# Both matrix products of each gated MLP by Strassen's seven half-size products, in a two-layer decoder step

## The chip, the cores and the metric

The kernel runs on one core of a Trainium2 chip. A core has five engines with a queue of instructions each: PE (matrix products, 128 by 128, results into PSUM), DVE (elementwise), ACT (elementwise with functions), POOL (elementwise, cannot read PSUM) and SP (issues DMA transfers). The metric is the device time of one execution in microseconds. Before the change it is 2903.1 us, the median of 3 runs (2901.17 to 2904.2).

## The reference

One inference step of two layers on 1024 prompt positions and 8 single-token samples, 1032 rows of 1024 features together, in float32. Layer 0 mixes positions with gated linear attention and sparse attention, layer 1 with an mLSTM. Behind each mixer stands the part that changes, a gated MLP with a causal convolution of width 3 on the gate:

```python
def _conv_ffn(xn, w_up, conv_w, conv_b, w_down, conv_state):
    t = xn.shape[1]
    gpre, up = jnp.split(xn @ w_up, 2, axis=-1)            # 1024 -> 2 x 2816
    full = jnp.concatenate([conv_state.astype(gpre.dtype), gpre], axis=1)
    acc = conv_b + full[:, 0:t] * conv_w[0]
    for j in range(1, CONV_W):
        acc = acc + full[:, j:j + t] * conv_w[j]
    h = jax.nn.gelu(acc) * up
    return h @ w_down, full[:, full.shape[1] - (CONV_W - 1):]  # 2816 -> 1024

xp = xp + d      # residual; at the end a final RMSNorm
```

## The kernel before, in words

The stream x is kept transposed: 8 tiles of 128 features by 1032 columns (1024 prompt positions and 8 samples), each as a pair `xh`, `xl` (a high part that PE takes as float32r, and the rest). A product of float32 numbers is made of three: high weight by high x, high by low, low by high. `product_steps` (L250) issues them for each 128-row block k of the input: 3 parts times 3 column groups of 344 (`GW`), so 9 matmuls per block.

`ffn` (L398) goes through the 22 inner feature tiles f. For each it makes the gate tile (72 matmuls of 344 columns), applies the convolution (L428 on ACT, L429 and L430 on DVE), the GELU (L432, L433 on ACT) and the factor `rstd` of the RMSNorm (L435 on POOL), then makes the up tile (72 matmuls) and multiplies it in (L440), and splits the result into `hh` and `hl` (L443, L444). Behind every 4 (or 3) inner tiles stands the down product of these: 8 output tiles, each added to `acc` (L458). In layer 1 the last 3 inner tiles are done by `finish` (L519), column group by column group, with the final norm and the output behind each.

A weight tile of 128 output columns is fetched on SP's queue (`load_w`, L223), multiplied by the norm's gain on POOL (L235, up weights only), and split into a high part on ACT (L236) and a low part on DVE (L237). `wraw` and `wspl` have two buffers each. PSUM holds two buffers of three banks for the products (`fpp`) and two banks for small things (`fpm`).

Each mixer ends in `out_project` (L358), whose output tile m is added to the stream (L392, L394) and split again by `split_x` (L343), which also squares it on ACT; `add_sq` (L166) sums the squares on POOL, and `make_rstd` (L189) makes `rstd` of the sum within the first gate tile's work.

The order on each queue is not that of the program text: a planner orders the traced instructions of each engine by their place in the text and by when it takes them to be ready. It places semaphore waits for every true dependence, for tile buffers too. Instructions of one engine then run in the planned order.

Of the kernel before, what the change touches and what calls it, by code (L numbers as in the profile page):

```python
# [14 lines left out]
PSUM = bass.MemoryType.PSUM  # L15

T = 1024
NS = 8
# [7 lines left out]
EPS = 1e-6  # L26

# [16 lines left out]
def grp(ap):  # L44
    return ap.rearrange("p (g t) -> p g t", g=NG)


class Trunk:
# [22 lines left out]
    def setup(self):  # L71
        nc, a = self.nc, self.a
        self.const = c = self.pool("const", 1)
        self.xp = self.pool("xp", 1)
# [10 lines left out]
        self.xh = [self.xp.tile([128, TT], F32R, name=f"xh{k}") for k in range(KD)]  # L85
        self.xl = [self.xp.tile([128, TT], F32R, name=f"xl{k}") for k in range(KD)]
        self.rstd = self.vec.tile([128, TT], F32, name="rstd")
        self.gains = c.tile([128, 56], F32, name="gains")

# [76 lines left out]
    def add_sq(self, sq, k):  # L166
        nc = self.nc
        if k == 0:
            self.sq = self.vec.tile([128, TT], F32, name="sq")
            nc.gpsimd.tensor_copy(self.sq, sq)  # L170
        else:
            (nc.vector if k == KD - 1 else nc.gpsimd).tensor_tensor(self.sq, self.sq, sq, op=OP.add)
# [67 lines left out]
    def project(self, pp, w, xh, xl, m=128):  # L240

        pt = pp.tile([128, NG, 512], F32, name="pp")
        self.products([pt[:m, g, :GW] for g in range(NG)], w, xh, xl)
        return pt

    def products(self, outs, w, xh, xl, ks=None):
        for _ in self.product_steps(outs, w, xh, xl, ks):
            pass

    def product_steps(self, outs, w, xh, xl, ks=None):  # L250
        nc = self.nc
        wh, wl = w
        kt = len(xh)
        for k in range(kt):
            kw = ks[k] if ks else k
            for i, (l, r) in enumerate(((wh, xh), (wh, xl), (wl, xh))):
                for g in range(NG):
                    nc.tensor.matmul(outs[g], l[:, kw, :], r[k][:, g * GW:(g + 1) * GW],  # L258
                                     start=(k == 0 and i == 0), stop=(k == kt - 1 and i == 2))
            if k < kt - 1:  # L260
                yield

    def stacked_steps(self, outs, w, xh, xl):

        nc = self.nc
        for k in range(KD):
            for m, x in ((128, xh), (64, xl)):
                for g in range(NG):
                    nc.tensor.matmul(outs[g][:m], w[:, k, :m], x[k][:, g * GW:(g + 1) * GW],  # L269
                                     start=(k == 0 and m == 128), stop=(k == KD - 1 and m == 64), skip_group_check=True)  # L270
            if k < KD - 1:
                yield
# [70 lines left out]
    def split_x(self, k, x):  # L343
# [5 lines left out]
        self.add_sq(x, k)  # L349
# [8 lines left out]
    def out_project(self, w, split, ks, ready, late, nat=None):  # L358
# [3 lines left out]
        with self.tp(name="opp", bufs=2, space=PSUM) as pp, \  # L362
# [15 lines left out]
            head = [begin(0)]  # L378
            self.take(head[0][1], ready)
            head.append(begin(1))  # L380
# [7 lines left out]
            for m in range(KD):  # L388
                pt, steps = head[m] if m < 2 else begin(m)
                self.take(steps, KD)  # L390
                x = self.rstd if m % 2 else self.vec.tile([128, TT], F32, name="sq_t")
                nc.vector.tensor_tensor(grp(x), pt[:, :, :GW], grp(self.xh[m].bitcast(F32)), op=OP.add)  # L392
                eng = nc.vector if m == KD - 1 else nc.gpsimd
                eng.tensor_tensor(x, x, self.xl[m].bitcast(F32), op=OP.add)  # L394
                self.split_x(m, x)


    def ffn(self, l, last):  # L398
        nc, a, tc = self.nc, self.a, self.tc
        parts = (4, 4, 4, 4, 3, 3)  # L400
        gain = self.gains[:, 16 + 8 * l:24 + 8 * l]
        w_up, w_dn = a["ffn_w_up"][l], a["ffn_w_down"][l]
        with self.tp(name="facc", bufs=1) as fa, self.tp(name="fh", bufs=5) as fh, \
                self.tp(name="ft", bufs=2) as ft, self.tp(name="f1", bufs=1) as f1:
            acc = [fa.tile([128, TT], F32, name=f"acc{m}") for m in range(KD)]
            with self.tp(name="fpp", bufs=2, space=PSUM) as pp, self.tp(name="fpm", bufs=2, space=PSUM) as self.ps:
                f0 = 0
                for pi, n in enumerate(parts):
                    hh, hl = [], []
                    final = last and pi == len(parts) - 1  # L410
                    if final:
                        spare = [(fh.tile([128, TT], F32R, name="hh"), fh.tile([128, TT], F32R, name="hl")) for _ in range(2)]
                    w = w_dn[f0 * 128:(f0 + n) * 128]
                    for f in range(f0, f0 + n):
                        pg = self.project(pp, self.split_w([(0, w_up[:, f * 128:(f + 1) * 128])], KD, gain), self.xh, self.xl)
                        if f == 0:
                            self.make_rstd(self.bank)
                            taps, st, cvp, cvs = self.conv_setup(l, f1)
                        g = ft.tile([128, 2 + T + 3 * NS], F32, name="g")
                        gs = g[:, 2 + T:].rearrange("p (b j) -> p b j", j=3)  # L420
                        nc.gpsimd.memset(g[:, 0:2], 0.0)
                        nc.gpsimd.tensor_copy(gs[:, :, 0:2], st[:, :, :, f])
                        self.scale_cols(g[:, 2:2 + T], gs[:, :, 2], pg)
                        nc.gpsimd.tensor_copy(cvp[:, :, f], g[:, T:T + 2])
                        nc.gpsimd.tensor_copy(cvs[:, :, :, f], gs[:, :, 1:3])
                        n3 = T + 3 * NS
                        h = ft.tile([128, n3], F32, name="cv")
                        nc.scalar.activation(h, g[:, 0:n3], AF.Identity, bias=taps[:, 66 + f:67 + f], scale=taps[:, f:f + 1])  # L428
                        nc.vector.scalar_tensor_tensor(h, g[:, 1:1 + n3], taps[:, 22 + f:23 + f], h, op0=OP.mult, op1=OP.add)  # L429
                        nc.vector.scalar_tensor_tensor(h, g[:, 2:2 + n3], taps[:, 44 + f:45 + f], h, op0=OP.mult, op1=OP.add)  # L430
                        u = ft.tile([128, TT], F32, name="u")
# [4 lines left out]
                        pu = self.project(pp, self.split_w([(0, w_up[:, DFF + f * 128:DFF + (f + 1) * 128])], KD, gain),  # L436
                                          self.xh, self.xl)
                        if final and f == f0 + n - 1:
                            wts = [self.last_weight(w, n, m, spare[m // 2]) for m in range(4)]
                        nc.vector.tensor_tensor(grp(u), pu[:, :, :GW], grp(u), op=OP.mult)  # L440
                        th = fh.tile([128, TT], F32R, name="hh")
                        tl = fh.tile([128, TT], F32R, name="hl")
                        nc.scalar.activation(th, u, AF.Copy)  # L443
                        nc.vector.tensor_tensor(tl, u, th, op=OP.subtract)  # L444
                        hh.append(th)
                        hl.append(tl)
                    if final:
                        break
                    for m in range(KD):
                        if (pi, m) == (len(parts) - 1, 5):  # L450
                            self.conv_store(l, cvp, cvs, ft)
                        pt = self.project(pp, self.split_w([(0, w[:, m * 128:(m + 1) * 128])], n), hh, hl)
                        ga = grp(acc[m])
                        if pi == 0:
                            nc.vector.tensor_tensor(ga, pt[:, :, :GW], grp(self.xh[m].bitcast(F32)), op=OP.add)
                            nc.gpsimd.tensor_tensor(acc[m], acc[m], self.xl[m].bitcast(F32), op=OP.add)
# [1494 lines left out]
```

## Time and profile before

| | before |
|---|---|
| median of 3 runs | 2903.1 us |
| profiled execution | 2923.18 us, span 2921.4 us |
| PE busy | 2843.8 us (97%), 17827 matmuls |
| DVE, ACT, POOL busy | 1394.3, 855.8, 788.7 us |
| mean granted clock of PE | 0.991 |
| layer 0's MLP | about 904 to 1674 us |
| layer 1's MLP with the final norm | about 2152 to 2921 us |

All times of the profile are of the one profiled execution, in microseconds from the span's start. Busy times of an engine are unions of its instructions; matmuls overlap each other in them, so the pace of a stream of matmuls is read from starts, not from durations.

### The profile page before, as it was taken

To read this page: it belongs to the slowest core of one execution; us is meant where nothing else is said; L and a number is where in the kernel's file an instruction comes from. 1 tells how busy PE (TensorE), PEld (TensorE's weight loads), DVE (VectorE), ACT (ScalarE), POOL (GpSimd) and SP (SyncE) were. 2 spreads that over 40 slices of the span, in tenths; PEclk is the share of its full clock that TensorE was granted. 3 is DMA by queue.
4 is the path that set the end of the run, shared out by engine and by line. 5 is a ranking of instruction groups with operands and counts; after the bars stand their busy time and mean duration, and the time that the engine had idled before them with its cause. 6 is when DMAs were issued, how large, how long until landed. Compare 5 with 4: busy or idle time off the path is not lost.

```text
span 2921.4 us, 41871 instructions
## 1 busy us (share of the span) xinstructions
PE 2843.8 (97%) x17827; PEld 2592.8 (89%) x17827; DVE 1394.3 (48%) x2111; ACT 855.8 (29%) x1353; POOL 788.7 (27%) x623
## 2 busy tenths in 40 slices
PE   7899999999999999999999999999999999999999
PEld 7677544687799999999999998889999999999998
DVE  6456775447555333433333764435553433333335
ACT  4333444333443221212122422323432212121224
POOL 3430223431134241313122411110343413131223
PEclk9999999999899999999999999999999999999999
DMA  6420010551111121111111212221111112111112
GB/s 184 146 80 23 1 58 1 175 179 37 38 45 47 33 62 37 55 40 49 54 31 55 56 44 60 60 66 48 44 50 37 55 37 58 44 48 48 36 55 80
DMA packets 252478, 171.92 MB, mean 59 GB/s; under 512 B 28878, under 2 KB 240949, under 8 KB 252229
## 3 DMA queue, kind: packets, MB, share of 16 engines
q1 hardware_dynamic: 237692, 128.36, 15.2%
q0 software_dynamic: 9728, 33.56, 3.4%
q10 hardware_dynamic: 4872, 7.33, 0.7%
q8 instruction: 140, 2.29, 0.3%
q14 instruction: 46, 0.37, 0.0%
HBM read 156.02 MB, written 17.38 MB: 59 GB/s over the span
## 4 chain that ended last, share of the span: by engine, by line
PE 91%; DVE 5%; ACT 1%; issue 1%; DMA 1%; POOL 0%; another core or an unknown queue 0%; SPq 0%; DVEq 0%; ACTq 0%; POOLq 0%
PE pp L258 56%; PE ps L258 14%; PE ps L1059 2%; PE pd L258 2%; PE ps L814 1%; PE pd L962 1%; PE ps L535 1%; PE ps L802 1%; PE pd L1028 1%; PE pd L1029 1%; DVE wl L237 1%; PE ps L1211 1%; PE ps L1813 1%; PE ps L1220 1%; PE ps L269 1%
## 5 line engine op out<-in xcount | busy, mean ns | idle before, releaser
L236 ACT ACTIVATE wh<-wr 128x1024 fp32r<-128x1024 f32 (+2 forms) x240 | 213.3, 889 | 1066.0 <-PE pp L258 880.5
L235 POOL TENSOR_TENSOR wr<-wr,gains 128x1024 f32<-128x1024 f32 x132 | 257.3, 1950 | 856.3 <-issue 250.1
L258 PE MATMUL pp<-xh,wh 128*128 128x344 f32 x2112 | 448.4, 321 | 0.0
L258 PE MATMUL pp<-xl,wh 128*128 128x344 f32 x2112 | 448.2, 320 | 0.0
L258 PE MATMUL pp<-xh,wl 128*128 128x344 f32 x2112 | 446.4, 319 | 0.0
L258 PEld LDWEIGHTS pp<-xl,wh 128*128 128x128 f32 x2112 | 357.4, 189 | 0.0
L258 PEld LDWEIGHTS pp<-xh,wh 128*128 128x128 f32 x2112 | 355.5, 188 | 0.4
L258 PEld LDWEIGHTS pp<-xh,wl 128*128 128x128 f32 x2112 | 351.9, 188 | 0.0
L237 DVE TENSOR_TENSOR wl<-wr,wh 128x1024 fp32r<-128x1024 f32 (+2 forms) x238 | 267.6, 1124 | 10.5 <-ACT wh L236 10.4
L258 PE MATMUL ps<-xh,wh 128*128 128x344 f32 x960 | 224.5, 339 | 3.2 <-ACT wh L236 1.9
L258 PE MATMUL ps<-xl,wh 128*128 128x344 f32 x960 | 215.0, 327 | 1.1 <-issue 0.6
L258 PE MATMUL ps<-xh,wl 128*128 128x344 f32 x960 | 212.1, 326 | 2.6 <-DVE wl L237 1.4
L258 PE MATMUL pp<-hh,wl 128*128 128x344 f32 x984 | 208.0, 319 | 0.7 <-DVE wl L237 0.7
L258 PE MATMUL pp<-hl,wh 128*128 128x344 f32 x984 | 208.5, 320 | 0.0
L258 PE MATMUL pp<-hh,wh 128*128 128x344 f32 x984 | 207.7, 320 | 0.0
L469 DVE TENSOR_TENSOR g<-pp,rstd 128x688 f32<-128x688 f32 x44 | 38.5, 875 | 311.1 <-PE pp L258 310.9
L458 DVE TENSOR_TENSOR acc<-pp,acc 128x1032 f32<-128x1032 f32 x72 | 88.7, 1232 | 196.8 <-PE pp L258 196.8
L440 DVE TENSOR_TENSOR u<-pp,u 128x1032 f32<-128x1032 f32 x44 | 54.2, 1232 | 257.0 <-PE pp L258 238.3
L258 PEld LDWEIGHTS ps<-xh,wh 128*128 128x128 f32 x960 | 163.5, 192 | 11.3 <-issue 6.0
L258 PEld LDWEIGHTS ps<-xl,wh 128*128 128x128 f32 x960 | 164.9, 192 | 6.6 <-issue 5.6
L258 PEld LDWEIGHTS ps<-xh,wl 128*128 128x128 f32 x960 | 163.5, 191 | 5.7 <-issue 3.6
L258 PEld LDWEIGHTS pp<-hh,wl 128*128 128x128 f32 x984 | 164.6, 188 | 1.2 <-DVE wl L237 1.2
(704 smaller groups left out, 4483.6 us busy)
## 6 DMA issues: line engine op xcount, KB each, us to landing
wr<-in_ffn_w_up_dram SPq DMA_DIRECT2D x88, 512.0 KB
wr<-in_ffn_w_down_dram SPq DMA_DIRECT2D x64, 256.0 KB
wr<-in_odd_w_in_dram SPq DMA_DIRECT2D x24, 512.0 KB
wr<-in_even_w_in_dram SPq DMA_DIRECT2D x18, 512.0 KB
wr<-in_ffn_w_down_dram SPq DMA_DIRECT2D x32, 192.0 KB
kv<-in_cache_win_kv_dram SPq DMA_DIRECT2D x8, 512.0 KB
cst<-in_state_mlstm_c_dram SPq DMA_DIRECT2D x16, 256.0 KB
out_dram<-cst SPq DMA_DIRECT2D x16, 256.0 KB
```

Of the source, the lines that this page charges most:

```text
L235: self.gain_eng.tensor_tensor(raw, raw, gain[:, :, None].to_broadcast([128, kt, m]), op=OP.mult)
L236: nc.scalar.activation(wh, raw, AF.Copy)
L237: nc.vector.tensor_tensor(wl, raw, wh, op=OP.subtract)
L258: nc.tensor.matmul(outs[g], l[:, kw, :], r[k][:, g * GW:(g + 1) * GW], start=(k == 0 and i == 0), stop=(k == kt - 1 and i == 2))
L269: nc.tensor.matmul(outs[g][:m], w[:, k, :m], x[k][:, g * GW:(g + 1) * GW], start=(k == 0 and m == 128), stop=(k == KD - 1 and m == 64), sk ...
L440: nc.vector.tensor_tensor(grp(u), pu[:, :, :GW], grp(u), op=OP.mult)
L458: nc.vector.tensor_tensor(ga, pt[:, :, :GW], ga, op=OP.add)
L469: nc.vector.tensor_tensor(dst[:, :2 * GW].rearrange("p (g t) -> p g t", g=2), pt[:, :2, :GW], self.rstd[:, :2 * GW].rearrange("p (g t) -> ...
L535: nc.tensor.matmul(pt, l[:, k, :], r[k][:, s], start=(k == 0 and i == 0), stop=(k == n - 1 and i == 2))
L802: nc.tensor.transpose(pt[:, j * 128:(j + 1) * 128], kv[:, half * 4 + j, sl * 256 + c * 128:sl * 256 + c * 128 + 128], self.ident)
L814: nc.tensor.matmul(hid[c][64 * h:64 * h + 64, :273], wt[:, c, q], xt[h][:, q, :273], start=(g == 0 and q == 0), stop=(g == 7 and q == 3))
L1059: nc.tensor.matmul(po[64 * g:64 * g + 64], v[:, kb, 64 * g:64 * g + 64], p[:, g * 512:(g + 1) * 512], start=first, stop=last)
```

## The change

Each MLP product is cut in two along inputs, outputs and columns, and done by Winograd's form of Strassen's algorithm: seven products of halves instead of eight. The columns are two halves of `HW` = 516, each two matmuls of `QW` = 258. One unit of weights makes one gate tile and its up tile (or the output tiles j and j+4): `factors` fetches both weight tiles, makes seven combined weights of half the rows and splits each in its high and low part, into a ring of five buffers. `combine` makes the seven combinations of x, once for each layer, into 28 slots that take the place of `xh`, `xl`. The seven products accumulate in three PSUM pairs of banks in the order a, b, a, b, c, b, c:

```diff
+    def combine(self, i, b, slot, pool):
+        b11, b12, b21, b22 = b
+        eng = nc.gpsimd if pool else nc.vector
+        if i == 1:
+            eng.tensor_tensor(b12, b22, b12, op=OP.subtract)
+            eng.tensor_tensor(b11, b11, b12, op=OP.add)
+        elif i == 4:
+            eng.tensor_tensor(b21, b21, b11, op=OP.subtract)
+            eng.tensor_tensor(b11, b22, b11, op=OP.subtract)
+        src = self.halves((b11, b11, b21, b12, b11, b21, b22)[i])
+        nc.scalar.activation(slot[:, 0, :, :QW], src, AF.Copy)
+        (nc.gpsimd if pool == 2 else nc.vector).tensor_tensor(slot[:, 1, :, :QW], src, slot[:, 0, :, :QW], op=OP.subtract)
+
+    def factors(self, srcs, kt, gain):
+        raws = [p.tile([128, KD, 128], F32, name=x)[:, :2 * kt] for p, x in ((self.wraw, "wr"), (ext, "wr2"))]
+        for raw, src in zip(raws, srcs):
+            nc.sync.dma_start(raw, src.rearrange("(k p) f -> p k f", p=128))
+        yield
+        if gain is not None:
+            for raw in raws:
+                nc.gpsimd.tensor_tensor(raw, raw, gain[:, :, None].to_broadcast([128, 2 * kt, 128]), op=OP.mult)
+        (a11, a12), (a21, a22) = ((r[:, :kt], r[:, kt:]) for r in raws)
+        ...
+        yield parts(a11)          # parts: high on ACT, low on DVE, kt x 128 columns each
+        nc.gpsimd.tensor_tensor(s1, a21, a22, op=OP.add)
+        nc.gpsimd.tensor_tensor(s2, s1, a11, op=OP.subtract)
+        yield parts(s2)
+        yield parts(a12)
+        nc.gpsimd.tensor_tensor(a11, a11, a21, op=OP.subtract)
+        yield parts(a11)
+        yield parts(s1)
+        yield parts(a22)
+        nc.gpsimd.tensor_tensor(a12, a12, s2, op=OP.subtract)
+        yield parts(a12)
+
+    def seven(self, pp, stream, rhs, after):
+        banks = {}
+        for i, x in enumerate("ababcbc"):
+            while len(self.ahead) < 4:
+                ...                                  # the next weights of the stream
+            hi, lo = self.ahead.popleft()
+            new = x not in banks
+            if new:
+                banks[x] = pp.tile([128, 2, 512], F32, name=f"pp{x}", bufs=1)
+            pt, right = banks[x][:, :, :QW], rhs(i)
+            for k, r in enumerate(right):
+                for n, (w, part) in enumerate(((hi, 0), (hi, 1), (lo, 0))):
+                    for q in range(2):
+                        nc.tensor.matmul(pt[:, q], w[:, k], r[:, part, q, :QW], start=(new and k == 0 and n == 0), ...)
+            after(i, pt)
```

All 22 inner tiles come first now. `t` and `u2` are the halves of one tile that is allocated once for the MLP. What follows the seven products of tile f:

```diff
+                def begin():
+                    ...
+                    nc.vector.tensor_tensor(self.halves(g[:, 2:2 + HW]), c11, self.halves(self.rstd[:, :HW]), op=OP.mult)
+                def after(i, pt):
+                    if i == 0:
+                        nc.scalar.copy(self.halves(t), pt)
+                        ...                          # f == 0: make_rstd
+                    elif i == 1:
+                        v.tensor_tensor(self.halves(u2), pt, self.halves(t), op=OP.add)
+                    elif i == 2:
+                        c11 = pt
+                    elif i == 3:
+                        u3 = self.vec.tile([128, TT], F32, name="sq")[:, :HW]
+                        v.tensor_tensor(self.halves(u3), pt, self.halves(t), op=OP.add)
+                    elif i == 4:
+                        v.tensor_tensor(self.halves(u3), pt, self.halves(u3), op=OP.add)
+                    elif i == 5:
+                        v.tensor_tensor(self.halves(t), pt, self.halves(t), op=OP.add)
+                    if i == (2 if f else 6):
+                        begin()
+                    if i == 6:
+                        v.tensor_tensor(self.halves(u2), pt, self.halves(u2), op=OP.add)
+                        nc.gpsimd.tensor_tensor(g[:, 2 + HW:2 + T], u2[:, :T - HW], self.rstd[:, HW:T], op=OP.mult)
+                        nc.gpsimd.tensor_tensor(gs[:, :, 2], u2[:, T - HW:], self.rstd[:, T:], op=OP.mult)
                         ...                          # convolution and GELU as before: ACT, DVE, DVE, ACT
                         nc.gpsimd.tensor_tensor(u, u, self.rstd, op=OP.mult)
+                        v.tensor_tensor(u[:, :HW], u[:, :HW], t, op=OP.mult)
+                        v.tensor_tensor(u[:, HW:], u[:, HW:], u3, op=OP.mult)
+                        nc.sync.dma_start(hid[f], u)
```

The inner tiles go to DRAM (`hid`) and come back as chunks of 6, 6, 6 and 4 tiles (layer 1: 6, 6, 6, and the last 4 in `finish`); the stream itself goes to DRAM (`res`) in `out_project` and comes back ahead of the down products. `turn` combines a chunk: for the first chunk within the last inner tile, for the others within the last output pair of the chunk before.

```diff
+            def first(i):                            # combinations of x, within f == 0
+                for j in range(4):
+                    self.combine(i, xs[j], right[4 * i + j], j < 3)
+                return right[4 * i:4 * i + 4]
+            def turn(i, n):
+                comb[i] = [self.slot(6 + 3 * i + p) for p in range(n // 2)]
+                for p in range(n // 2):
+                    self.combine(i, quads(raw[p], raw[p + n // 2]), comb[i][p], 1 + p // 2)
...
+            for c, (f0, n) in enumerate(chunks):
+                ...
+                for j in range(4):
+                    ...
+                    def after(i, pt):
+                        if i == 0:
+                            nc.scalar.copy(self.halves(t), pt)
+                        elif i == 1:
+                            v.tensor_tensor(self.halves(u2), pt, self.halves(t), op=OP.add)
+                            p.tensor_tensor(u2, u2, a12, op=OP.add)
+                        elif i == 3:
+                            v.tensor_tensor(self.halves(u3), pt, self.halves(t), op=OP.add)
+                            p.tensor_tensor(u3, u3, a22, op=OP.add)
+                            p.tensor_tensor(t, t, a21, op=OP.add)
+                        else:
+                            to, x = {2: (a11, a11), 4: (a22, u3), 5: (a21, t), 6: (a12, u2)}[i]
+                            v.tensor_tensor(self.halves(to), pt, self.halves(x), op=OP.add)
+                        if j == 3 and nxt and not (last and c == len(chunks) - 1):
+                            turn(i, nxt[1])
+                    self.seven(pp, stream, lambda i: used[i], after)
...
+            self.open_x()                            # layer 0: xh, xl are made again behind the MLP
+            for m in PAIRS:
+                self.split_x(m, big[:, m])
```

One tile `big` of 8 by 1032 columns holds the stream, the MLP's work areas, and the buffers that the mixers had in tiles of their own (`oN`, `oT`, `kv`, `nat`, `p` and others). The order of the stream's tiles in `out_project` and behind layer 0's MLP is `PAIRS` = 0, 4, 1, 5, 2, 6, 3, 7.

## Rows read from the trace of the kernel before

**Rows 1.** The page: busy times; the chain of work that ended last, by engine.
```profile
PE 2843.8 (97%) x17827; PEld 2592.8 (89%) x17827; DVE 1394.3 (48%) x2111; ACT 855.8 (29%) x1353; POOL 788.7 (27%) x623
PE 91%; DVE 5%; ACT 1%; issue 1%; DMA 1%; POOL 0%; another core or an unknown queue 0%; SPq 0%; DVEq 0%; ACTq 0%; POOLq 0%
```
**Rows 2.** Windows of both MLPs: length, busy per engine (instructions), clock, DMA share, GB/s.
```profile
903.80:1674.00 770.20, 766.14 (x4831) 763.50 (x4830) 327.82 (x328) 175.55 (x203) 213.01 (x175) 1.00 0.17 48
2152.00:2921.00 769.00, 762.64 (x4842) 759.03 (x4841) 319.62 (x375) 180.52 (x233) 209.71 (x173) 1.00 0.17 50
```
**Rows 3.** Timeline of PE, matmuls of 344 columns, 39 from first to last row.
```profile
1395.42 0.63 PE L258 MATMUL pp<-xl,wh 128*128 128x344 f32 x3
...
1401.58 0.64 PE L258 MATMUL pp<-xh,wl 128*128 128x344 f32 x3
```
**Rows 4.** Timeline of PE, matmuls of 264 columns, 7 from first to last row.
```profile
2904.87 0.28 PE L535 MATMUL ps<-hl,xh 128*128 128x264 f32 x1
...
2905.72 0.29 PE L535 MATMUL ps<-hh,xl 128*128 128x264 f32 x1
```
**Rows 5.** Timeline of one gate tile: next product's first matmul, then what follows.
```profile
963.21 0.64 PE L258 MATMUL pp<-xh,wh 128*128 128x344 f32 x3
...
963.41 0.88 DVE L469 TENSOR_TENSOR g<-pp,rstd 128x688 f32<-128x688 f32 x1 [7.69 <-PE pp L258]
...
964.81 1.27 ACT L428 ACTIVATE cv<-g,taps 128x1048 f32<-128x1048 f32 x1 [0.81 <-DVE g L472]
...
966.11 1.31 DVE L429 SCALAR_TENSOR_TENSOR cv<-g,taps,cv 128x1048 f32<-128x1048 f32 x1 [0.21 <-ACT cv L428]
...
970.04 2.41 POOL L435 TENSOR_TENSOR u<-u,rstd 128x1032 f32<-128x1032 f32 x1 [0.88 <-ACT u L433]
```
**Rows 6.** Lines by form: elementwise instructions, busy and mean ns.
```profile
L440 DVE TENSOR_TENSOR u<-pp,u 128x1032 f32<-128x1032 f32 x44 | 54.2, 1232 | 257.0 <-PE pp L258 238.3 <-POOL u L435 18.6
L471 DVE TENSOR_TENSOR g<-pp,rstd 128x336 f32<-128x336 f32 x44 | 21.9, 497 | 0.0
L1085 POOL TENSOR_TENSOR co<-co,cf 128x512 f32<-128x512 f32 x8 | 10.2, 1277 | 61.0 <-DVE cf L1083 61.0
L235 POOL TENSOR_TENSOR wr<-wr,gains 128x1024 f32<-128x1024 f32 x14 | 26.7, 1904 | 36.9 <-DMA wr<-in_ffn_w_up_dram 32.0 <-issue 3.5 <-DVE u L440 1.4
```
**Rows 7.** Source L237 and L236, 1000 to 1040 us: ns min/median/max.
```profile
L237 DVE TENSOR_TENSOR wl<-wr,wh x7: 679/682/2736, 1004.3 to 1038.5; 128x512 fp32r<-128x512 f32 x6, 128x1024 fp32r<-128x1024 f32 x1
L236 ACT ACTIVATE wh<-wr x7: 632/632/1060, 1002.7 to 1036.9; 128x512 fp32r<-128x512 f32 x6, 128x1024 fp32r<-128x1024 f32 x1
```
**Rows 8.** Timeline of DVE and POOL; source L444, L440: ns min/median/max.
```profile
937.56 1.90 POOL L235 TENSOR_TENSOR wr<-wr,gains 128x1024 f32<-128x1024 f32 x1 [1.36 <-DVE u L440]
938.60 1.95 DVE L444 TENSOR_TENSOR hl<-u,hh 128x1032 fp32r<-128x1032 f32 x1 [1.13 <-ACT hh L443]
L444 DVE TENSOR_TENSOR hl<-u,hh x44: 1232/1234/2010, 938.6 to 2870.4; 128x1032 fp32r<-128x1032 f32 x44
L440 DVE TENSOR_TENSOR u<-pp,u x44: 1232/1232/1233, 936.2 to 2868.1; 128x1032 f32<-128x1032 f32 x44
```
**Rows 9.** Timeline of PE where the first MLP's `rstd` is made.
```profile
915.33 1.32 PE L196 MATMUL ps<-sq,ones 128*128 128x344 f32 x4
916.23 0.90 PE L258 MATMUL pp<-xh,wh 128*128 128x344 f32 x3
...
917.93 0.84 PE L196 MATMUL ps<-sq,ones 128*128 128x344 f32 x2
```
**Rows 10.** PE's longest wait of layer 1, and the windows around it.
```profile
1706.13 0.90 PE L1775 MATMUL ps<-ident,sq_t 128*128 128x128 f32 x3 [3.21 <-DVE sq_t L309]
...
1700.00:1710.00 10.00, 6.79 (x38) 6.34 (x37) 9.94 (x31) 1.65 (x5) 0.00 (x0) 0.83 0.00 0
1710.00:1720.00 10.00, 10.00 (x66) 10.00 (x65) 6.13 (x10) 4.24 (x4) 1.90 (x1) 1.00 0.28 73
```
**Rows 11.** The window with the most DMA traffic of 540 to 660 us.
```profile
600.00:610.00 10.00, 9.31 (x84) 7.24 (x84) 6.41 (x17) 1.07 (x2) 4.11 (x5) 1.00 0.76 260
```

More of the change, by code (lines that the diff above doesn't have):

```diff
@@ new lines, in factor_stream @@
+    def factor_stream(self, units):
+        units = list(units)
+        next(units[0])
+        for i, u in enumerate(units):
+            if i + 1 < len(units):
+                next(units[i + 1])
+            yield from u
+    def seven(self, pp, stream, rhs, after):
+        nc = self.nc
+        banks = {}
+        for i, x in enumerate("ababcbc"):
+            while len(self.ahead) < 4:
+                nxt = next(stream, None)
+                if nxt is None:
+                    break
+                self.ahead.append(nxt)
+            hi, lo = self.ahead.popleft()
[6 more added lines that the diff above has]
+                    for q in range(2):
+                        nc.tensor.matmul(pt[:, q], w[:, k], r[:, part, q, :QW], start=(new and k == 0 and n == 0),
+                                         stop=(k == len(right) - 1 and n == 2), skip_group_check=True)
+            after(i, pt)
@@ L398, in ffn @@
     def ffn(self, l, last):
-        nc, a, tc = self.nc, self.a, self.tc
-        parts = (4, 4, 4, 4, 3, 3)
+        nc, a, tc, big = self.nc, self.a, self.tc, self.big
         gain = self.gains[:, 16 + 8 * l:24 + 8 * l]
         w_up, w_dn = a["ffn_w_up"][l], a["ffn_w_down"][l]
[L403 to L415, printed above, removed]
@@ new lines, in ffn @@
+        pools = [self.tp(name="fr", bufs=1, side="right"), self.tp(name="fx", bufs=1, side="right"),
+                 self.tp(name="fl", bufs=1)]
+        self.fr, self.fx, self.fl = (p.__enter__() for p in pools)
+        right = [self.slot(i) for i in range(8)] + [None] * 20
+        for i in range(27, 7, -1):
+            right[i] = self.slot(i)
+        hid = self.dram.tile([NF, 128, TT], F32, name="hid")
+        chunks = ((0, 6), (6, 6), (12, 6)) + (() if last else ((18, 4),))
+        ups = [self.factors([w_up[:, c + f * 128:c + f * 128 + 128] for c in (0, DFF)], 4, gain) for f in range(NF)]
@@ L481, in conv_setup @@
+        while pools:
+            pools.pop().__exit__(None, None, None)
+        if not last:
+            self.open_x()
+            self.order = PAIRS
+            for m in PAIRS:
+                self.split_x(m, big[:, m])
+    def conv_setup(self, l, taps, st, rows):
+        nc, a = self.nc, self.a
         nc.sync.dma_start(rows[0:66, 0], a["ffn_conv_w"][l].rearrange("j (f p) -> (j f) p", p=128))
@@ L788, in nsa_compress @@
         for g in range(8):
[L789 removed]
+            kv = two[g % 2]
             for b in range(NS):
```

281 lines of the change are left out of this document (170 added, 111 removed).

## The prediction

> **What bounds the kernel now.** I read the busy times first, then the chain of work that ended last, then each MLP's window. PE is busy 97% of the span and makes 91% of the chain [rows 1]; within each MLP it is idle for 4 and 6 us of 770 [rows 2]. DVE, ACT and POOL work for 43%, 23% and 28% of that time in the first. So an MLP lasts as long as its matmuls, and all elementwise work is hidden. The change cuts matmul columns and adds elementwise work and dependences; the question is what stays hidden.
>
> **PE's stream.** Starts of 344-column matmuls are 6.16/39 = 0.158 us apart [rows 3], those of 264 columns 0.85/7 = 0.1214 [rows 4]: 0.459 and 0.460 ns a column. The weight load of each matmul is hidden at both, so I take 0.1185 us for 258 columns. Layer 0 before: 22 x 144 up and 1584 down matmuls, 4752 x 0.1579 = 750 us. After: 22 x 7 products x 4 blocks x 6 = 3696 up and 4 x 7 x 11 block pairs x 6 = 1848 down, 5544 x 0.1185 = 657. Layer 1: 4536 x 0.1579 + 72 x 1032 columns x 0.459 ns = 750; after 5208 x 0.1185 + 96 x 1032 x 0.459 ns = 663, its last chunk being four tiles in place of three. Sum: **-181 us**.
>
> The Trainium skill, page "TensorE: Matmul & The Clock Gate", section "Back-to-back issue gap", gives N/2.4 ns and 2.5 ns for a warm matmul; by that the term would be an estimated -160. Rows 3 and 4 show no such constant, and their pace is what I use.
>
> **The wait that each inner tile adds.** The gate's second half comes from the seventh product. Only then follow: DVE's sum into `u2`, POOL's product with `rstd`, the convolution, the GELU, POOL's `rstd` again, and `u` times `t`. `t` is one buffer, so the next tile's copy into `t` (ACT, behind product 0) waits for that multiplication; and product 2 adds onto the bank that this copy reads, so PE waits for the copy. From the end of product 6:
> - 0.2 until DVE starts [rows 5], 0.69 for 516 columns out of PSUM (between 0.497 for 336 and 1.232 for 1032 [rows 6])
> - 1.28 for POOL's 508 columns (1.277 for 512 [rows 6]) and 0.2 for the samples' eight
> - 7.64 from ACT's start on the convolution to the end of POOL's factor (964.81 to 970.04 + 2.41 [rows 5])
> - 0.68 for `u` times `t` (DVE, 512 columns, two SBUF inputs), 0.63 for ACT's copy [rows 7], 0.2 for four hand-overs
>
> That is 11.5 us. A product takes 24 x 0.1185 = 2.84. Products 0 and 1 of the next tile run meanwhile. So does product 4, on the free third bank pair, if the planner draws it ahead; that it reorders PE's queue is seen where eight up matmuls stand before the last of L196 [rows 9]. All other products are held. Then come 2 and 3, the evacuation that product 5 waits for (0.2 + 0.69 + 0.1), 5 and 6: a period of 11.5 + 5.7 + 1.0 + 5.7 = 23.9 us against 19.9 of matmuls (before: 144 x 0.158 = 22.7). Without product 4 drawn ahead it is 11.5 + 5 x 2.84 = 25.7.
>
> **What delays that chain.** DVE instructions with both inputs in SBUF and POOL's do not run side by side: the subtraction that began at 938.60 while POOL worked until 939.46 took 1.95 us, as long as POOL's rest and most of its own 1.23; the multiplication that reads PSUM took 1.232 to 1.233 us in all 44 cases [rows 8]. For one inner tile POOL has two gains of 1.90, five sums or products of 1.28 (all new to it) and one of 2.41, together 12.6; DVE has seven low parts of 0.68, two convolution steps of 1.31 and two products of 0.68, together 8.7. That is 21.3 us one after the other, more than PE's 19.9. The chain holds most of these steps, the rest falls into its gaps, and none is interrupted. I take one gain (1.90) and one low part (0.68) ahead of steps of the chain: 23.9 + 2.6 = 26.5 us. Below: 23.9, all conflicts hidden. Above: 28.3, the same delay without product 4. Idle: 44 x (26.5 - 19.9) = **+290 us**.
>
> **The combinations.** They share that pair of engines.
> - Start of each MLP: `first` makes 28 low parts on DVE (19.0), 12 sums on POOL (15.4) and 4 on DVE (2.7), 37 us, nearly all before the first tile's seventh product. A period of 26.5 leaves 5 free and some 5 can be done ahead: 25 a layer, **+50** (10 to 74). Before, `split_x` lay under the out projection and the first gate tile.
> - From up to down: `turn` for six tiles has seven times two low parts on DVE and one on POOL (18.5) and 12 sums (15.4): 34 us. The last inner tile leaves 5 and 3.8 (no gains follow), the first pair of outputs 3.6 of its 14.9 (low parts 3.6, sums 3.8, evacuations 3.8): 21 a layer, **+43** (0 to 68).
> - Between chunks the same 34, less 3.8 done ahead and 7 that two pairs leave free, less 5 of weight work that can wait: 18, four times; 8 for the chunk of four: **+80** (20 to 110).
> - Behind layer 0's MLP six tiles are split after the last product (ACT 1.06 twice a tile), and `finish` prepares weights late: **+10** (0 to 20).
>
> **What costs nothing, I take.** The transfers of `hid` and `res` are 60 of 0.53 MB a layer: 32 MB, 122 us at the 260 GB/s of [rows 11], beside 800 us. Queued on SP they stand between weight fetches, whose cover is four parts ahead in the ring; if the 14 tiles that return ahead of the down products (7.4 MB, 28 us) hold the weights up, it is +28 a layer. In the mixers buffers change place: 0 (-6 to +6).
>
> **Sum.** -181 + 290 + 50 + 43 + 80 + 10 = +292: 2923.2 + 292 = 3215 in the profiled execution. That stood 0.7% above the median of the runs, so **3195 us**.
>
> **Rivals.**
> - *The chain stays covered* (the other side): PE finds matmuls for its wait, the idle time goes, and half of the combinations' 183 stay: 2923 - 181 + 92 = 2834, in the runs 2815. For it: the reordering of [rows 9]. Against: three bank pairs, two of them held, leave one product. It decides if PE's idle time per tile is under about 2 us: then the two savings outweigh the rest. 11%, a part of which (2%) ends within 0.2%.
> - *Only the dependence counts*: 23.9 and half the combinations: 2923 - 181 + 176 + 92 = 3010, in the runs 2989. For it: DVE has gaps of several us within the chain that the small work fits. 21%.
> - *The clock falls in each tile*: behind a wait of 3.21 us PE's granted clock was 0.83 in that window of 10 us and 1.00 in the next [rows 10], which is 3.4 us at 1.2 GHz, 1.7 us of matmuls lost. The wait here is 23.9 + 2.6 - 19.9 = 6.6 us a tile. At each of 44 tiles and 7 boundaries: +87, 3302, in the runs 3279. Against: the waits may be cut by single matmuls. 24%.
> - *Product 4 is not drawn ahead and the returning tiles hold up the weights*: 28.3 a tile (+79) and +56: 3350, in the runs 3327. 8%.
>
> The same page of the Trainium skill, section "HAM oscillation — how this bites in real kernels", says that PE left idle between bursts starts each burst cold. By it the third rival would be the likeliest; the trace has waits like the one in rows 10 too rarely to show what repeated ones do.
>
> That the change does not shorten PE's stream at all gets no chance, since 264 columns take 0.77 of the time of 344 [rows 3, 4].
>
> **How the numbers follow.** The forecast (3100 to 3260) gets 36%. 2980 to 3330 leaves out the first rival (11%) and the far ends of the others. A measurement tells 0.2% of this kernel from no change: slower in all cases but the first, 89%; faster 9%; same 2%.
>
> **What would show it.** PE busy near 83% of the span; its largest wait in the MLPs for ACT's copy into `t`, 44 times, 4 us or more each; copies into `t` 26 to 27 us apart; product 4's matmuls ahead of product 2's; POOL's 512-column sums often longer than 1.28; the first inner tile near 50 us; DVE and POOL waiting at the chunks while PE stands. It is wrong if PE stays above 92% in the up part, or if the copies are about 20 us apart: then the chain is not what I took it for.

## The result, and the profile after

The changed kernel takes 3389.6 us (median of 4 runs, 3387.5 to 3393.1) where the kernel before takes 2902.1 beside it: a ratio of 1.1685 [1.1664, 1.1706]. Slower was forecast, but 3195 and at most 3330. The profiled execution has a span of 3390.2 us, 469 more than that of before (2921.4).

Busy times and the chain of work that ended last, by engine, on the page of the kernel after (the profile follows this chain back only to about 2400 us, so its shares can't be held against those of before):

```profile
PE 2864.6 (84%) x19363; PEld 2589.8 (76%) x19363; DVE 1957.0 (58%) x2805; ACT 1081.3 (32%) x1893; POOL 1536.9 (45%) x1213
PE 13%; POOL 6%; DVE 5%; ACT 2%; issue 2%; DMA 1%; DVEq 0%; POOLq 0%; SPq 0%; ACTq 0%
```

Against [rows 1]: PE has an eighth fewer columns in the MLPs (5544 x 258 against 4752 x 344 in layer 0) and yet is busy 21 us longer. A busy time that does not fall with the work says that the work ran slower. Windows of the kernel after (as in [rows 2]: length, busy time of PE, PEld, DVE, ACT and POOL, granted clock, DMA): 19 inner tiles of layer 0, then the same 19 of layer 1, the start of the first MLP, the turn from up to down, and one chunk boundary.

```profile
958.57:1508.88 550.31, 431.26 (x3192) 426.66 (x3192) 305.65 (x323) 137.13 (x209) 281.18 (x244) 0.86 0.17 55
2457.90:3008.59 550.69, 431.63 (x3192) 427.03 (x3192) 305.27 (x323) 137.16 (x209) 280.86 (x244) 0.85 0.17 55
876.70:958.57 81.87, 44.69 (x250) 40.70 (x250) 65.31 (x69) 32.17 (x52) 48.37 (x36) 0.74 0.17 48
1538.91:1583.76 44.85, 26.49 (x154) 25.44 (x154) 31.27 (x34) 16.63 (x31) 38.01 (x30) 0.71 0.40 127
1628.45:1683.45 55.00, 37.60 (x254) 36.39 (x253) 35.73 (x39) 18.29 (x36) 45.49 (x33) 0.84 0.28 87
```

An inner tile takes 550.31/19 = 28.96 us where the forecast was 26.5. PE's clock was 1.00 in both MLPs before; here it is 0.86 among the inner tiles and lower at every stage's edge. The waits of the kernel after (us in total, times, longest):

```profile
PE ppa L512 <- ACT tu L567: 280.4, 42, 12.8
ACT tu L567 <- DVE sq_t L599: 196.5, 42, 8.9
DVE sq_t L599 <- POOL sq_t L598: 136.2, 41, 8.2
```

Read downward, this is the forecast chain backward: PE waits for ACT's copy into `t`, that for DVE's `u` times `t`, that for POOL's product with `rstd`. One tile of it, timeline of the kernel after, from its product 6:

```profile
1114.96 3.04 PE L512 MATMUL ppc<-s,wx 128*128 128x258 f32 x24
...
1117.84 2.07 PE L512 MATMUL ppa<-s,wh 128*128 128x258 f32 x16
1118.04 0.70 DVE L586 TENSOR_TENSOR tu<-ppc,tu 128x516 f32<-128x516 f32 x1 [1.46 <-PE ppc L512]
...
1118.82 1.78 POOL L587 TENSOR_TENSOR big<-tu,rstd 128x508 f32<-128x508 f32 x1 [7.74 <-DVE tu L586]
...
1120.80 1.26 ACT L592 ACTIVATE big<-big 128x1048 f32<-128x1048 f32 x1 [2.06 <-POOL big L588]
...
1122.64 3.04 PE L512 MATMUL ppc<-s,wx 128*128 128x258 f32 x24
...
1126.50 2.36 POOL L598 TENSOR_TENSOR sq_t<-sq_t,rstd 128x1032 f32<-128x1032 f32 x1 [0.60 <-ACT sq_t L596]
1128.82 1.89 POOL L458 TENSOR_TENSOR wr<-wr,gains 128x1024 f32<-128x1024 f32 x1
1128.89 2.37 DVE L599 TENSOR_TENSOR sq_t<-sq_t,tu 128x516 f32<-128x516 f32 x1 [3.06 <-POOL sq_t L598]
...
1131.29 0.59 ACT L567 COPY tu<-ppa 128x516 f32<-128x516 f32 x1 [4.35 <-DVE sq_t L599]
...
1131.93 5.53 PE L512 MATMUL ppa<-s,wh 128*128 128x258 f32 x24 [6.26 <-ACT tu L567]
...
1137.04 3.42 PEld L512 LDWEIGHTS ppb<-s,wl 128*128 128x128 f32 x24
1137.26 3.41 PE L512 MATMUL ppb<-s,wl 128*128 128x258 f32 x24
```

Three things are to be seen. Product 4 (at 1122.64) runs ahead of product 2 (at 1131.93). The chain, from PE leaving product 6 at 1117.84 to 1131.93, is 14.1 us, to the tenth what was forecast (11.5 + 2.6). Most of the price is where it was put: DVE's multiplication starts 0.07 us behind a gain on POOL and takes 2.37 in place of 0.68, and POOL's product behind a low part on DVE takes 1.78 in place of 1.28. The last 0.4 lies between the convolution and the GELU's factor, and that the tenth fits is luck. And product 2 behind the wait takes 5.3 us, from 1131.93 to 1137.26, where product 6 takes 2.88. The windows around the wait, PE alone (length, busy, granted clock, DMA):

```profile
1118.00:1125.60 7.60, 7.60 (x65) 1.00 0.03 10
1125.60:1131.90 6.30, 0.08 (x1) 0.68 0.53 157
1131.90:1135.30 3.40, 3.37 (x15) 0.50 0.38 155
1135.30:1138.70 3.40, 3.40 (x20) 0.59 0.00 0
1138.70:1142.00 3.30, 3.30 (x29) 1.00 0.00 0
```

At full clock until the wait, at 0.50 (1.2 GHz) behind it, back at 1.00 some 6 us later. From 1131.93 to the next product 6's end (1147.31) PE needs 15.4 us (14.4 in the tile before), not the 12.4 forecast: 14.1 + 15.4 and 14.1 + 14.4 are the 29.5 and 28.5 between which the tiles alternate. The Trainium skill, page "TensorE: Matmul & The Clock Gate", section "HAM oscillation — how this bites in real kernels", says that repeated idle stretches make each burst start cold; the 0.50 agrees.

### The profile page after: what moved, and what is told of

It is laid out like the page before. It is cut to its first block, busy times and chain, and to the rows that moved or that the text cites. A ratio compares the mean times of both kernels' runs of the same rounds, so it can differ in the third digit from the quotient of the medians.

```text
span 3390.2 us, 47830 instructions
## 1 busy us (share of the span) xinstructions
PE 2864.6 (84%) x19363; PEld 2589.8 (76%) x19363; DVE 1957.0 (58%) x2805; ACT 1081.3 (32%) x1893; POOL 1536.9 (45%) x1213
## 5 line engine op out<-in xcount | busy, mean ns | idle before, releaser
L512 PE MATMUL ppa<-s,wl 128*128 128x258 f32 x1254 | 207.4, 330 | 125.9 <-ACT tu L567 115.7
L512 PE MATMUL ppa<-s,wh 128*128 128x258 f32 x1212 | 198.8, 329 | 123.8 <-ACT tu L567 114.6
L512 PEld LDWEIGHTS ppa<-s,wl 128*128 128x128 f32 x1254 | 196.5, 237 | 131.1 <-ACT tu L567 119.1
L512 PEld LDWEIGHTS ppa<-s,wh 128*128 128x128 f32 x1212 | 188.6, 236 | 128.7 <-ACT tu L567 118.0
L512 PE MATMUL ppb<-s,wh 128*128 128x258 f32 x1824 | 252.4, 295 | 37.2 <-DVE rstd L663 12.4
L512 PE MATMUL ppb<-s,wl 128*128 128x258 f32 x1848 | 252.8, 294 | 25.7 <-DVE sq L576 6.2
L512 PEld LDWEIGHTS ppb<-s,wh 128*128 128x128 f32 x1824 | 240.0, 201 | 42.2 <-issue 13.6
L512 PEld LDWEIGHTS ppb<-s,wl 128*128 128x128 f32 x1848 | 241.8, 200 | 28.6 <-DVE sq L576 6.4
L512 PE MATMUL ppc<-s,wh 128*128 128x258 f32 x1254 | 169.2, 291 | 21.4 <-DVE big L668 19.4
L512 PE MATMUL ppc<-s,wl 128*128 128x258 f32 x1206 | 162.5, 291 | 17.0 <-DVE big L668 15.3
```

The costliest lines, as they stand in the source:

```text
L512: nc.tensor.matmul(pt[:, q], w[:, k], r[:, part, q, :QW], start=(new and k == 0 and n == 0), stop=(k == len(right) - 1 and n == 2), skip_g ...
```

## The experiments

All are edits of the changed kernel; ratios are to the kernel before, run beside them. My theory: the chain through `t` holds PE; DVE and POOL delay the chain and the edges of the stages by excluding one another; and each of these waits costs PE its clock as well. "Period" is the distance of the copies into `t` from tile 2 to tile 20.

**1. PE kept busy in the wait.** With seven products in the order 0, 1, 4, 2, 3, 5, 6 as the planner had them:

```diff
+for _ in range(52):
+    nc.tensor.matmul(pad[:, :QW], x[:, :128], x[:, :QW], start=True, stop=True)
```

> 52 matmuls of 258 columns whose result nobody reads are put into PE's queue of every inner tile but the first, behind product 4 and ahead of product 2, where PE now waits 6.3 us for the copy into t; the order of all else in PE's queue stays. They take 52 x 0.1185 = 6.2 us, so PE has work throughout the wait. Theory 'the clock falls in each tile': behind the wait products 2 and 3 took 4.9 and 3.0 or 5.5 and 3.4 us in place of 2.84 each, and the granted clock of the up part is 0.84; with the wait filled the products are back at 2.84, the copies into t stand 26.4 to 26.9 us apart in place of 29.0, and the kernel takes 42 x 2.3 = 97 us less: about 3290, though PE does 44 x 6.2 us more work. Rival 'the products behind the wait are slow for another reason' (their weights or their right-hand parts come late): the products stay at 4.9 to 5.5 us, the copies stay 29 us apart or move further apart, 3390 to 3410.

Measured: 3347.5 us, ratio 1.1484 [1.1455, 1.1513]; period 27.3. Its window from tile 2 to tile 20, and the products behind the wait:

```profile
1006.10:1498.10 492.00, 486.43 (x3976) 479.23 (x3976) 299.32 (x307) 130.21 (x198) 283.93 (x236) 1.00 0.19 59
1253.62 3.14 PE L516 MATMUL ppa<-s,wl 128*128 128x258 f32 x24
1257.00 3.14 PE L516 MATMUL ppb<-s,wh 128*128 128x258 f32 x24 [0.24 <-DVE tu L580]
```

The clock is 1.00 and the product behind the wait takes 3.1 us where it took 5.5, so added work made the kernel faster: the clock theory holds. The size was missed. The period fell by 1.65 us, not 2.3, since the slow product had hidden DVE's sum into `u2`, for which PE now waits. And in experiments 1 to 4 the first copy of the program came 15 to 24 us later than in the changed kernel (917.4 here, 895.4 there), behind the first mixer, which no edit touched; the kernel before took 2913.5 us beside them, 11 more than beside the changed kernel, so the edits need not be the reason. From that copy to the end it is 2428 us against 2495: 67 less, close to 42 x 1.65 = 69.

**2. A second buffer for `t`.**

```diff
+t = t0 if f == 0 or f % 2 else flat[:, 3200:3200 + HW]
```

> Tiles 2, 4, ..., 20 copy product 0 into another buffer than the tiles on either side, so that copy no longer waits for the multiplication of the tile before; nothing is left out. Theory 'the one buffer t holds PE': the wait of 6.3 us and the slow products behind it go. What is late next is DVE's sum into u3 behind product 3, which waits until u3 has been multiplied into u (16 us after product 6); products 0 to 4 fill 14.2 us of that. Period about 16.7 + 5.7 = 22.4, at most 24: 42 x 5 to 6.6 us less, 3110 to 3180. Rival 'DVE and POOL are the bound': they need 21.3 us a tile one after the other and each hand-over costs, so the period stays above 26 and the time above 3270.

Measured: 3221.9 us, 1.1057 [1.1030, 1.1085]; periods 23.7 and 24.0, as the first theory said, and the next wait is the one it named:

```profile
1268.07 4.62 PE L512 MATMUL ppb<-s,wh 128*128 128x258 f32 x24 [1.91 <-DVE sq L578]
1272.53 3.03 PE L512 MATMUL ppc<-s,wl 128*128 128x258 f32 x24
```

A wait of 1.91 us, and again the 24 matmuls behind it take 4.46 us, from start to start. The time is 42 us above the theory's range all the same: the first copy comes 15 us later, and the turn from the up to the down part takes 54 us in both layers in place of 45 and 43.

**3. `rstd` ahead of the chain.**

```diff
 elif i == 4:   # u3 complete
+    nc.gpsimd.tensor_tensor(u3, u3, self.rstd[:, HW:], op=OP.mult)
 elif i == 5:   # t complete
+    nc.gpsimd.tensor_tensor(t, t, self.rstd[:, :HW], op=OP.mult)
-nc.gpsimd.tensor_tensor(u, u, self.rstd, op=OP.mult)   # behind the GELU
```

> t and u3 are multiplied by rstd as soon as they are complete (two POOL products of 516 columns, behind products 4 and 5), in place of the product of 1032 columns behind the GELU; the result is the same but for rounding, POOL's work is the same within 0.2 us. Theory 'the chain from product 6 to the copy into t sets the period': it loses the 2.36 us of that step and the 1.7 us that DVE's multiplication by t then lost beside POOL's next instruction: 14.0 becomes about 10, the period 29.0 becomes 24.9 (22.9 if PE's wait, then 2 us, no longer costs it the clock): 3120 to 3215. Rival 'the shared pair DVE and POOL is the bound': same work, same period, 3370 to 3400.

Measured: 3207.2 us, 1.1005 [1.0966, 1.1044]; period 24.0. The same work in another place gives 5 us a tile, so the chain and not the load of the two engines sets the period here. The multiplication is down to 0.70, PE's wait to 2.07, and the clock is lost all the same:

```profile
1263.13 0.70 DVE L600 TENSOR_TENSOR sq_t<-sq_t,tu 128x516 f32<-128x516 f32 x1 [0.52 <-ACT sq_t L597]
...
1264.51 4.66 PE L512 MATMUL ppa<-s,wx 128*128 128x258 f32 x24 [2.07 <-ACT tu L567]
```

**4. No gains on POOL.**

```diff
-ups = [self.factors([...], 4, gain) for f in range(NF)]
+ups = [self.factors([...], 4, None) for f in range(NF)]
```

> The up weights are not multiplied by the norm's gain (left out: 88 POOL products of 1.90 us, 3.8 us a tile). Theory 'POOL's and DVE's instructions that exclude one another lengthen the chain': the gain that starts behind POOL's rstd product keeps DVE's multiplication by t at 2.37 us in place of 0.68; without it, unless the next sum of POOL takes its place, the chain loses up to 1.7 us: period 27.3 to 28, 3315 to 3350, of which 4 to 8 at the two starts. Rival 'only the dependence counts': 3380 to 3395, since none of these 88 instructions is a step of the chain.

Measured: 3345.5 us, 1.1489 [1.1450, 1.1528]; period 27.9, and 7 to 10 us less from the first copy to the second. Instructions that are no step of the chain lengthen it. POOL's next sum takes the gain's place, so a part stays:

```profile
1269.31 1.26 POOL L472 TENSOR_TENSOR s<-wr 128x512 f32<-128x512 f32 x1
1269.38 1.73 DVE L599 TENSOR_TENSOR sq_t<-sq_t,tu 128x516 f32<-128x516 f32 x1 [3.07 <-POOL sq_t L598]
```

**5. All sums, and all low parts, on DVE.** In `combine` and in `factors` (the first of the changed lines):

```diff
-eng = nc.gpsimd if pool else nc.vector
+eng = nc.vector
```

> All sums and low parts that make the combinations (of x, of the returning tiles) and the four sums of each weight go to DVE; POOL keeps the gains and the products with rstd. Theory 'DVE's two-input SBUF instructions and POOL's run one after the other': then what counts is their sum, and POOL takes 1.28 us for what DVE does in 0.68. A chunk boundary (12 sums and 7 low parts on POOL, 24 us) needs 11 us less, the start 7 less, the tile's chain the same: 6 boundaries x 11 + 2 x 7 = 80 less, 3300 to 3330. Rival 'they work side by side and the split over two engines is what hides the combinations': DVE, the busier one (58% of the span), becomes the bound at the boundaries and gets four more instructions a tile: 3390 to 3430.

Measured: 3270.5 us, 1.1264 [1.1239, 1.1290]: 119 less, more than expected. The period stays 29.0. The two pairs of output tiles around a chunk boundary take 21.2 and 20.2 us in place of 31.5 and 23.5, the turn 30.5 in place of 44.9. The low parts of the returning tiles (count, ns min/median/max), first at a boundary of the changed kernel, on DVE and POOL:

```profile
L447 DVE TENSOR_TENSOR s<-s,s x14: 697/1108/1777, 1627.7 to 1661.7; 128x516 fp32r<-128x516 f32 x14
L447 POOL TENSOR_TENSOR s<-s,s x7: 1182/1654/1674, 1631.5 to 1661.2; 128x516 fp32r<-128x516 f32 x7
```

and at the same boundary of this kernel:

```profile
L447 DVE TENSOR_TENSOR s<-s,s x21: 679/684/697, 1598.8 to 1626.2; 128x516 fp32r<-128x516 f32 x21
```

Side by side both engines look busy and each is stretched by the other; one alone does all 21 in 0.68 us each. The Trainium skill, page "Trainium Architecture — The Big Picture", section "What this means for kernel authors", calls the pair's port an exclusive lock and not a split of bandwidth; this agrees.

**6. Experiments 2 and 3 together.**

```diff
+t = t0 if f == 0 or f % 2 else flat[:, 3200:3200 + HW]
...
+nc.gpsimd.tensor_tensor(t, t, self.rstd[:, :HW], op=OP.mult)
-nc.gpsimd.tensor_tensor(u, u, self.rstd, op=OP.mult)
```

> The second buffer for t and the early multiplication by rstd together. No wait for the chain is left in PE's queue. Theory 'then the shared pair DVE and POOL is the bound' (21.3 us a tile as predicted, 12.6 on POOL and 8.7 on DVE): copies into t 22 to 23 us apart, 3080 to 3130. Rival 'then PE is the bound': 19.9 to 20.5 us apart, the granted clock of the up part at 1.00, 2990 to 3020. Second rival 'the two do the same thing': 23.5 to 24 as with either alone, 3180 to 3210.

Measured: 3154.2 us, 1.0870 [1.0842, 1.0898]; period 23.4, clock 0.98 in the up part. That lies between the first theory's numbers and the second rival's; PE now waits for DVE's `u3`, and the run alone doesn't say whether load or order is behind that. The next does. Its window from tile 2 to tile 20, and that wait in both layers:

```profile
973.10:1394.70 421.60, 379.59 (x3020) 370.51 (x3019) 261.38 (x306) 124.35 (x199) 279.04 (x252) 0.98 0.23 68
PE ppc L512 <- DVE sq L580: 69.4, 40, 3.3
```

Forty waits of 1.7 us on average left the clock at 0.98: not every short wait costs it.

**7. Both, with the sums on DVE and the gain in x.** Edits 2, 3 and 5, and

```diff
+for k in PAIRS:
+    nc.scalar.activation(big[:, k], big[:, k], AF.Identity, scale=gain[:, k:k + 1])
```

> As the run with the second buffer and the early factor, and the sums and low parts on DVE, and the gain multiplied into x once a layer (8 ACT instructions on tiles of 1032 columns) in place of 44 weights. POOL is left with 4 us a tile, DVE has 16.3, of which 11.5 exclude POOL: 15.5 for the pair, under PE's 19.9. Theory 'the pair set the pace': copies 20 to 20.7 us apart, start 15 us shorter each, boundaries 11 shorter: 3390 - 44 x 8.5 - 30 - 66 = 2920 (2890 to 2960). Rival 'DVE's queue holds PE by its order, whatever the load': 22 us or more, 3000 to 3080.

Measured: 2920.9 us, 1.0069 [1.0043, 1.0095]. From tile 2 to tile 20 PE doesn't stop:

```profile
954.80:1316.90 362.10, 361.93 (x3019) 361.73 (x3018) 281.60 (x378) 127.97 (x200) 111.80 (x144) 1.00 0.27 80
```

The period is 20.1: 362.1/3024 = 0.1197 us a matmul is the pace at last, and with the same buffers as in 6 it was the two engines' work that had been in the way: in such a window POOL is busy 112 us in place of 279, DVE 282 in place of 261. Which of the moved sums, low parts and gains did most of it, this run doesn't say.

**8. Plain products, new mixers.** The MLP and out projection of the kernel before in the changed kernel (the first pair of lines is against the changed kernel, the second against the kernel before).

```diff
-self.seven(pp, stream, rhs, after)
+pg = self.project(pp, self.split_w([(0, w_up[:, f * 128:(f + 1) * 128])], KD, gain), self.xh, self.xl)
...
-acc = [fa.tile([128, TT], F32, name=f"acc{m}") for m in range(KD)]
+acc = [self.big[:, m] for m in range(KD)]
```

> The changed kernel with the MLP and the out projection of the kernel before: eight full products, the inner features in SBUF, the hidden state's sum in the shared tile; only the mixers' buffers stay changed. It measures what the mixers gave: by the traces the first out projection ends at 876.7 in place of 904.0 and the second mixer is 5 us shorter: 27 to 32 us under the kernel before beside it. Rival 'that was the order of the whole program, which any edit moves': in four edited kernels the first copy into t came 15 to 24 us later than in the changed one; then 5 to 15 us under the kernel before.

Measured: 2890.5 us, 0.9953 [0.9938, 0.9968]: 13 under the kernel before, within the rival's range; that the order of the program is the reason isn't shown. Windows of the first 200 us, of this kernel and of the kernel before:

```profile
0.00:200.00 200.00, 183.33 (x1280) 157.78 (x1281) 121.00 (x245) 83.70 (x139) 88.02 (x102) 0.98 0.51 152
```

```profile
0.00:200.00 200.00, 168.97 (x1124) 139.15 (x1125) 107.66 (x220) 74.83 (x128) 78.24 (x89) 0.98 0.50 148
```

The mixers gained there, but the profiled execution of before is itself 20 us over its median, so the 27 us between the traces are not all the change's.

**9. Seven products in the up part alone.** As 7, with full matmuls of 344 columns in the down parts (1584 in layer 0; 1512 and the finish in layer 1).

```diff
+nc.sync.dma_start(raw, hid[f])              # raw is lo's own buffer
+nc.scalar.activation(hi, raw, AF.Copy)
+nc.vector.tensor_tensor(lo, raw, hi, op=OP.subtract)
```

> The up product as in the run with the second buffer, the early factor, the sums on DVE and the gain in x; the down product back to eight full products: the inner features come back from DRAM, are split in the spare buffers, and 4752 less 3168 = 1584 matmuls of 344 columns (1512 and the finish's in the second layer) replace 1848 of 258. Theory 'the seven products of the down part do not pay': in the run with them the copy of tile 21 stood 292 us ahead of the layer's last product and 219 of that were matmuls; now it is 14 for the rest of the tile, 250 of matmuls and about 2: 26 less in layer 0, 19 less in layer 1: 2876 (2862 to 2895), and under the run with plain products throughout (2890) by 5 to 25. Rival 'the split and the transfers of the returning tiles hold PE up too, with waits that cost it the clock': 2900 or more.

Measured: 2904.0 us, 1.0022 [1.0011, 1.0034]: the theory's 2876 missed, the rival's side. PE's longest waits for these tiles and for the finish:

```profile
PE pp L649 <- ACT hh L632: 22.0, 3, 17.7
PE ps L714 <- ACT fh L267: 11.4, 1, 11.4
```

**10. The same, with the returning tiles earlier.** And the weights of the finish are prepared during the part before; the lines show the first of the two edits.

```diff
-for i in range(27, 7, -1):
+for i in range(8, 28):          # slots of products 2, 3 come free first, and lie where the tiles return to
     right[i] = self.slot(i)
```

> As the run with seven products in the up part alone, with the returning tiles placed where the buffers of products 0 to 3 come free, so that they can load before the last inner tile ends, and the weights of the finish prepared during the part before. In the run before this one PE waited 17.7 us for the first returning tile in layer 1, about 9 in layer 0, and 11.4 for the finish's first weight. Theory 'these waits are what is left': 25 to 35 us less, 2865 to 2880, under the kernel before by about 1% and under the run with plain products (2890). Rival 'the transfers themselves are late (res and hid share the queue at the turn)': 2890 to 2905, the waits stay at the same place.

Measured: 2881.7 us, 0.9931 [0.9917, 0.9945]; the wait for the tiles is 11.4 us in four waits now, and the finish's is gone from the list. It is faster than both kernels, by 0.7% than the one before. That it is faster than 8 isn't shown: the intervals overlap.

**11. A quarter of the first combinations.**

```diff
-for j in range(4):
-    self.combine(i, xs[j], right[4 * i + j], j < 3)
+self.combine(i, xs[0], right[4 * i], True)
+right[4 * i + 1:4 * i + 4] = [right[4 * i]] * 3
```

> The changed kernel, but the first combinations are made for one of the four pairs of tiles and used for all four (left out: 21 of 28 low parts, 21 copies and 12 of 16 sums a layer). Theory 'the start is as long as the work of DVE's SBUF instructions and POOL's one after the other': by durations alone the window from the out projection's end to the second copy into t (81.9 us) holds 19 of low parts, 18 of sums, 5 of rstd, 32 of weight work for two to three tiles and 8 of the first chain: 82 in all. Less 14.3 + 13.3 it is 54: each start 25 to 28 us shorter, 3333 to 3342. Rival 'the start waits for rstd, for the weights' transfers or for the chain': 5 to 10 us a layer, 3370 to 3380.

Measured: 3329.6 us, 1.1477 [1.1456, 1.1497]: 60 less, where the theory said 48 to 57. First to second copy: 46.4 and 38.4 us in place of 63.2 and 61.9. From the out projection's end to the second copy it is 60.1 and 56.0 us in place of 81.9 and 81.3, which is 47 of the 60; most of the rest lies in the tiles behind, 28.7 us apart in place of 29.0, and why isn't shown. ACT's copies for these low parts are left out as well, so this run alone doesn't clear ACT.

## Why the prediction was wrong

The direction and the chain were right; four sizes were not. Forecast and measured, in the profiled executions:

| term | forecast | measured |
|---|---|---|
| PE's stream | -181 | -168 |
| 44 inner tiles | +290 | +391 |
| start of the MLPs | +50 | +97 |
| up to down | +43 | +57 |
| chunk boundaries | +80 | +108 |
| ends, finish, mixers | +10 | -14 |

The column adds up to 471 where the spans differ by 469. The sum is surer than its parts: PE waits for the copy 42 times and not 44, and by the trace the second to fourth lines are 525 together in place of 545 (twice 707.1 us from the out projection's end to the first copy of the down part, less 444.6 of matmuls), so that some 20 us more lie in the down parts. The last line is 27 (the first out projection ends at 876.7, not 904.0) against 13 more from the first MLP's last product to the end of the second out projection (behind the first MLP the split of x now stands open).

- **PE's stream**: 0.1197 us a matmul in place of 0.1185, by experiment 7. Small.
- **The inner tile**: 44 x (29.0 - 20.1), with the 0.1197 of the line above. The chain was right, product 4 ahead was right, the 2.6 for the shared pair was nearly right (2.2 are the pair's). What failed is "then come 2 and 3 ...: 5.7 + 1.0 + 5.7": those products were priced at full clock. They stand behind an idle stretch of 6.3 us, and the price of that was known: 1.7 a wait by [rows 10], which I put into a rival of 24%. It is 2.0 to 3.0 (14.4 and 15.4 in place of 12.4), and slow products stand behind all 42 waits. My reason against it, that single matmuls may cut the wait, fails in the trace (0.08 us busy in 6.30). Experiment 1 shows the cause, and a gain of 1.65 a tile when only that is mended.
- **The starts**: 81.9 and 81.3 us from the out projection's end to the second copy, where a running tile would take 33. I set 37 us of combinations against what a period leaves free. But nothing is in stock at a start: the same window holds the weights of two to three tiles (five gains, eleven sums) and the work on `rstd`: some 80 us of DVE's and POOL's instructions one after the other, as long as the window (an estimate from their counts in it and their undisturbed durations). Experiments 4, 5 and 11 shorten the two windows by 12 and 9, 13 and 10, 22 and 25 us; what they take out is about 9.5, 12 and 27.
- **Turn and boundaries**: the mechanism was right, the size too small. A boundary costs 24 or 20 us, not 18, and the chunk of four about 20, not 8; the clock in the window of a boundary is 0.84. For a chunk, POOL has 55 us (15 for residual sums, 16 for weights, 24 for the next tiles) and DVE's SBUF instructions 24: 79 where PE needs 60. Counting that sum against PE's time would have given 19 without any guess about what is done ahead, though not the 24.
- **The mixers**: 0 was forecast, 13 gained by experiment 8. The forecast's correction from the profiled time to the median took off 20 us where 3 were due: the profiled execution of before was long, that of after was not.

The third rival had the clock, but at 1.7 us a wait, and the edges at their forecast sizes (3279). With its wait at the measured 2.5 us and the upper bounds I had given (74, 68, 110), the sum would have been -181 + 290 + 110 + 74 + 68 + 110 + 10 = 481, or 3384 in the runs. That it comes so near is partly luck: the starts cost 97 and not 74, up to down 57 and not 68. The range stopped at 3330 because it treated the clock and the upper ends as alternatives; here they came together.

Most signs held: PE's largest wait on the copy into `t`, 42 times, product 4 ahead of product 2, POOL's sums at 1.6 to 1.7 at the boundaries. PE at 84% (83 forecast) held by luck: its busy time didn't fall by 181 us but rose by 21. The first inner tile took 63 us from copy to copy, not 50, and the copies 29 us apart in place of 26 to 27 were the sign that said which step was off.

## What to carry to other kernels

When a change trades PE columns for elementwise work, add DVE's two-input SBUF instructions and POOL's as one engine and hold that sum against PE's time for each stage, edges included; moving a sum from POOL to DVE can then be a gain although DVE is the busier one. Follow each buffer that a later tile overwrites to its last reader: the wait of one buffer cost 9 us a tile here, and a second buffer and one product moved off the chain gave 5.6 of it back. Price a wait of PE that comes back in each tile with the slow matmuls behind it: where it lasted 6 us, all 42 had them, so this was a sure cost and not a rival. Then look at the granted clock, since waits near 2 us had them in two kernels and mostly not in a third.

## What the runs showed of the hardware that was not expected

Waits of 1.91 and 2.07 us were enough to put the next 24 matmuls at 4.46 and 4.49 us in place of 2.9 (experiments 2 and 3), as after 6.26 us (5.3), while forty waits of 1.7 us on average left the clock at 0.98 (experiment 6). And matmuls that compute nothing paid for themselves: 52 in each tile, 6.2 us of PE, made the kernel 1.2% shorter.
